# An encoder layer's second MLP product: residual filled into the accumulators by ScalarE, shared accumulators kept by copies, a last half-pass without seven-product units, and a normalisation that ends from PSUM

## The chip, the cores and the metric

The kernel runs on one core of a Trainium2 chip. The metric is the device time of one execution in microseconds (us). The kernel before took 1088.08 us, the median of three runs (1086.86 to 1090.04).

Five queues matter here, and each works strictly in the order of its own instructions: TensorE (PE, matrix products into PSUM), VectorE (DVE), ScalarE (ACT), GpSimd (POOL) and SyncE (SP, which issues the loads). [...]

## The reference, cut to what matters

One layer of a post-norm encoder on 256 tokens of width 2048, all in float32. The change is in the last third:

```python
def squared_relu_mlp(h, w_mlp_in, w_mlp_out):        # 2048 -> 8192 -> 2048
    return jnp.square(jax.nn.relu(h @ w_mlp_in)) @ w_mlp_out

x = layer_norm(ALPHA * x + xa, ln2_g[l], ln2_b[l])
ff = squared_relu_mlp(x, w_mlp_in[l], w_mlp_out[l])
x = layer_norm(ALPHA * x + ff, ln3_g[l], ln3_b[l])
```

## The kernel before, in words

**Split operands.** Every float32 operand is used as a sum of two parts, `hi` and `lo`. ACT writes `hi` (a copy rounded to the PE's format), then DVE writes `lo` (source minus `hi`). One product is then three matmuls: hi x hi, hi x lo, lo x hi (`mm3`, lines 164 to 166). A stretch of up to 1024 weight columns that is split at once is called a *part* here (`part`, `queued_split`, lines 957 and 958). `w_hi` has four buffers and `lo` four, so ACT can split a part only when PE has finished the part four before it.

**The work list.** Two kinds of items, each with one 1 MB load of weights, form one list (`items`): a *tile* ("g") makes 128 of the hidden columns, and a *unit* ("u") multiplies 256 hidden rows (a pair of tiles) into 1024 of the 2048 output columns. `step` takes the next item and `fetch` issues a load three items ahead. A tile (`hidden_tile`) is two parts, T0 and T1, and 32 matmuls. Its bank is then emptied (ACT line 876, DVE line 877). After every second tile come ReLU and square on ACT, the split of the result ("ht", lines 880 and 881), and, where the pair is needed for a seven-product unit, sums of its quarters (DVE, lines 900 to 904) and their split ("aux"). That chain is `stages`; `late_finish` and `finish` decide where it stands, and for the last pair it is put in the queues exactly where `finish` is called.

**Units.** A unit is a 2 x 2 block product. A plain unit ("P") does eight block products, 24 matmuls of 512 columns, from two parts, P0 and P1. A seven-product unit ("S") does Strassen's scheme in Winograd's form, 21 matmuls from four parts, S0 to S3; three more DVE additions (`push_sums`, tile `s_t`) make sums of weights first. A P accumulates into the banks x11, x12, x21, x22; an S into x11, x12, x21 and four more, p1, p5, p6, p7. The products shared by several results stand in those four.

**Passes.** `UNITS` names the units of eight passes. A pass goes through one quarter of the hidden rows (16 tiles, index c) and half the output columns (index q), and q runs 0, 1, 1, 0, 0, 1, 1, 0, so that two neighbouring passes share the banks. Where q changes, the banks are *closed*: ACT copies p1 to `m_t` (line 1159), and DVE adds all banks, in up to eleven operations spread over the next parts, into the residual tiles `res` (lines 1118 to 1122), the first time with the factor ALPHA. x22 is added to `res` whenever a run of P units ends. In the last pass the last four units keep their parts, so that the first row block (tokens 0 to 127) finishes before the second.

**End.** `moments` gives mean and 1/sigma of a row block; then, for five column pieces each, DVE does (x - mean) x gain (line 1266), then x 1/sigma + bias (line 1274), and SP stores the piece.

What sets the order: inside the loop nearly all PE, ACT and DVE instructions are chained in the order in which the code calls them (`queue`); `after(n, f)` calls f when n more parts have been split. What stands outside (`free_order`: emptying a tile's bank, most `stages`) is placed by the scheduler when the program is built.

Of the kernel before, what the change touches and what calls it, by code (L numbers as in the profile page):

```python
# [38 lines left out]
def encoder_kernel(ctx: ExitStack, tc: tile.TileContext, t, out):  # L39
# [54 lines left out]
    def rsqrt(src, n, scale, eps):  # L94
        v = small.tile([P, 8], F32, tag="rs_v", name="rs_v")
        nc.vector.tensor_scalar(out=v[:, :n], in0=src, scalar1=scale, scalar2=eps,
                                op0=ALU.mult, op1=ALU.add)
# [1 line left out]
        nc.gpsimd.tensor_tensor(out=r[:, :n], in0=v[:, :n], in1=mhalf[:, :n], op=ALU.pow)
# [63 lines left out]
    def mm3(ps, ah, al, bh, bl, start, stop, keep=lambda ins: ins):  # L163
        keep(nc.tensor.matmul(ps, ah, bh, start=start, stop=False))  # L164
# [1 line left out]
        keep(nc.tensor.matmul(ps, al, bh, start=False, stop=stop))  # L166
# [359 lines left out]
    def moments(st):  # L526
        mv = small.tile([P, 2], F32, tag="mv", name="mv")
        nc.vector.bn_aggr(mv, st[0][:, :st[1], :])
# [556 lines left out]
    run = {}  # L1085

    def one_pass(n):
# [8 lines left out]
        if opens:
            cols = [slice((2 * q + i) * 512, (2 * q + i + 1) * 512) for i in range(2)]
            r11, r12, r21, r22 = run["res"] = [res[b][:, cc] for b in range(NB) for cc in cols]
            whole = units if closes else units + UNITS[n + 1]
# [3 lines left out]
            run["left"][id(x22)] = 2 * (n_p - HELD) if final else 2 * (len(whole) - len(whole.lstrip("P")))
            run["total"] = dict(run["left"])
            run["fresh"] = [r11, r12, r21, r22] if c == 0 else []
            run["s"] = run["sevens"] = n_s
        r11, r12, r21, r22 = run["res"]
        left, total, fresh = run["left"], run["total"], run["fresh"]

        def mm(ps, x, hi, lo):  # L1110
            start = left[id(ps)] == total[id(ps)]
            left[id(ps)] -= 1
            mm3(ps, *x, hi, lo, start, left[id(ps)] == 0, queue)

        def merge(r, x, op=ALU.add):
            if any(r is y for y in fresh):
                fresh[:] = [y for y in fresh if y is not r]
                return nc.vector.scalar_tensor_tensor(out=r, in0=r, scalar=ALPHA, in1=x, op0=ALU.mult, op1=op)
            return nc.vector.tensor_tensor(out=r, in0=r, in1=x, op=op)

        def more(ps, op=ALU.add):
            nc.vector.tensor_tensor(out=m_t, in0=m_t, in1=ps, op=op)

        def tile_bank(it):

            i = at[0] - 1
            near = [[x for x in part_ if x[0] == "u"][:1] for part_ in (items[:i][::-1], items[i:])]
            if all(x and is_seven(x[0]) for x in near) or it[1:] == (0, LEAD):
                return x22
            behind, ahead = [sum(x[0] == "g" for x in part_[:next(  # L1130
                (j for j, x in enumerate(part_) if is_seven(x) or x[1:] == (0, LEAD)), 0)])
                for part_ in (items[:i][::-1], items[i + 1:])]
            return p7 if behind == 1 and ahead else p6 if behind and not ahead else p1

        n_unit, parts = 0, []
        while n_unit < len(units):
# [6 lines left out]
            if p in sevens:  # L1143
                if run["s"] == run["sevens"] and not final:
                    while banks:
                        banks.popleft()()
# [11 lines left out]
                if run["s"] == 0:  # L1158
                    nc.scalar.activation(m_t, p1, AF.Copy)
                    xs_done = [lambda r=r, ps=ps: merge(r, ps) for r, ps in ((r12, x12), (r11, x11), (r21, x21))]  # L1160
                    banks.extend([lambda: merge(r11, m_t), lambda: more(p6)] + xs_done * (units[-1] == "S") + [
                        lambda: merge(r22, p5), lambda: merge(r12, p5),
# [232 lines left out]
```

## Time and profile before

| | |
|---|---|
| median of three runs | 1088.08 us |
| the profiled execution, its time | 1086.87 us |
| the profiled execution, its span | 1085.1 us |
| PE busy over the span | 1069.8 us |
| DVE busy | 948.0 us |
| ACT busy | 651.3 us |
| POOL busy | 37.3 us |

The span is the time from the first to the last instruction that the profile shows, and 1.8 us of the execution lie around it. An engine is "busy" while an instruction of it runs. A share over the whole span mixes stages, so the prediction reads the second product (from 445 us on) and the end apart.

### The profile page before, as it was taken

What the parts mean: (1) busy time and instruction counts of PE and PEld (TensorE: products, weight loads), DVE (VectorE), ACT (ScalarE), POOL (GpSimd) and SP (SyncE); (2) the same over time, 40 slices, a digit from 0 to 9 for tenths busy, and PEclk for the clock granted to TensorE, in tenths of its full rate; (3) what the DMA queues carried; (4) which work ended last, traced back from release to release, by engine and by line L of the source; (5) the groups of instructions that cost most, each with busy time, mean ns of one, the idle gap of its engine ahead of it and who ended that gap; (6) DMA issues with size and microseconds to landing.
All of it is one profiled execution on the core that took longest, in us unless ns stands there. A gap on an engine that the chain in (4) does not pass through costs nothing.

```text
span 1085.1 us, 15274 instructions
## 1 busy us (share of the span) xinstructions
PE 1069.8 (99%) x5828; PEld 925.4 (85%) x5828; DVE 948.0 (87%) x1314; ACT 651.3 (60%) x949; POOL 37.3 (3%) x43
## 2 busy tenths in 40 slices
PE   9999999999999999999999999999999999999995
PEld 6988899988999878888888888888888888888885
DVE  6878677778779686889999999989999999999998
ACT  6555567546575526566756667656676656676660
POOL 2402000000000000000000000000000000000000
PEclk9999999999999999999999999999999999999998
DMA  9664454476476435765564655646555555556552
GB/s 331 232 232 136 156 192 155 156 239 222 164 248 231 179 124 187 242 224 195 193 233 156 232 195 194 223 165 231 187 203 208 188 209 211 199 192 230 193 196 78
DMA packets 37369, 215.86 MB, mean 199 GB/s; under 512 B 4272, under 2 KB 5168, under 8 KB 13616
## 3 DMA queue, kind: packets, MB, share of 16 engines
q1 hardware_dynamic: 37296, 214.89, 56.0%
q8 instruction: 45, 0.74, 0.3%
q14 instruction: 28, 0.23, 0.1%
HBM read 212.78 MB, written 2.10 MB: 198 GB/s over the span
## 4 chain that ended last, share of the span: by engine, by line
PE 93%; DVE 3%; DMA 2%; issue 1%; ACT 0%; SPq 0%; POOL 0%; DVEq 0%; ACTq 0%
PE acc L1028 15%; PE acc L165 12%; PE acc L164 12%; PE acc L166 12%; PE acc L1036 8%; PE att L164 5%; PE att L166 5%; PE att L165 5%; PE att L1028 4%; PE acc L206 2%; PE acc L204 2%; PE acc L205 2%; PE att L1036 2%; PE acc L213 1%; PE att L213 1%; DMA raw<-in_w_qa 1%
## 5 line engine op out<-in xcount | busy, mean ns | idle before, releaser
L87 ACT ACTIVATE w_hi<-raw 128x1024 fp32r<-128x1024 f32 (+2 forms) x134 | 131.5, 989 | 110.0 <-PE acc L166 74.7
L88 DVE TENSOR_TENSOR w_lo<-raw,w_hi 128x1024 fp32r<-128x1024 f32 (+2 forms) x130 | 146.0, 1132 | 53.4 <-ACT w_hi L87 52.3
L1028 PE MATMUL acc<-x2t,w_hi 128*128 128x512 f32 x688 | 178.4, 391 | 0.0
L958 DVE TENSOR_TENSOR lo<-raw,w_hi 128x1024 fp32r<-128x1024 f32 (+1 forms) x150 | 164.0, 1114 | 4.1 <-ACT w_hi L957 3.8
L957 ACT ACTIVATE w_hi<-raw 128x1024 fp32r<-128x1024 f32 (+1 forms) x150 | 142.2, 972 | 15.0 <-PE att L1028 10.0
L1028 PEld LDWEIGHTS acc<-x2t,w_hi 128*128 128x128 f32 x688 | 126.6, 189 | 22.8
L958 DVE TENSOR_TENSOR lo<-s_t,w_hi 128x1024 fp32r<-128x1024 f32 x96 | 117.1, 1220 | 15.1 <-ACT w_hi L957 14.9
L957 ACT ACTIVATE w_hi<-s_t 128x1024 fp32r<-128x1024 f32 x96 | 101.5, 1057 | 42.5 <-DVE lo L958 18.7
L1036 PEld LDWEIGHTS acc<-x2t,lo 128*128 128x128 f32 x688 | 93.9, 190 | 6.7
L1036 PE MATMUL acc<-x2t,lo 128*128 128x256 f32 x688 | 95.9, 282 | 0.0
L876 ACT ACTIVATE tmp<-acc 128x256 f32<-128x256 f32 x47 | 17.7, 385 | 117.1 <-PE acc L1028 112.7
L165 PE MATMUL acc<-w_lo,xt 128*128 128x512 f32 (+2 forms) x192 | 69.6, 364 | 0.6 <-DVE w_lo L88 0.6
L166 PE MATMUL acc<-w_hi,xt 128*128 128x512 f32 (+2 forms) x192 | 69.2, 361 | 0.0
L164 PE MATMUL acc<-w_hi,ht 128*128 128x512 f32 x174 | 67.8, 390 | 0.0
L166 PE MATMUL acc<-w_hi,ht 128*128 128x512 f32 x174 | 67.7, 389 | 0.0
L165 PE MATMUL acc<-lo,ht 128*128 128x512 f32 x174 | 67.7, 389 | 0.0
L164 PE MATMUL acc<-w_hi,xt 128*128 128x512 f32 (+2 forms) x192 | 66.0, 363 | 0.3 <-ACT w_hi L87 0.3
L165 PE MATMUL att<-lo,aux 128*128 128x512 f32 x140 | 54.5, 389 | 0.0
L166 PE MATMUL att<-w_hi,aux 128*128 128x512 f32 x140 | 54.5, 389 | 0.0
L164 PE MATMUL att<-w_hi,aux 128*128 128x512 f32 x140 | 54.5, 389 | 0.0
L1028 PE MATMUL att<-x2t,w_hi 128*128 128x512 f32 x208 | 53.9, 392 | 0.0
L165 PE MATMUL acc<-w_lo,ot 128*128 128x512 f32 (+1 forms) x136 | 51.7, 381 | 0.0
(290 smaller groups left out, 2482.3 us busy)
## 6 DMA issues: line engine op xcount, KB each, us to landing
raw<-in_w_mo SPq DMA_DIRECT2D x38, 1024.0 KB, 4.8
raw<-in_w_mc SPq DMA_DIRECT2D x35, 1024.0 KB, 4.8
raw<-in_w_out SPq DMA_DIRECT2D x16, 1024.0 KB, 4.8
row_b<-in_w_mo SPq DMA_DIRECT2D x13, 1024.0 KB, 4.9
raw_x<-in_w_mo SPq DMA_DIRECT2D x13, 1024.0 KB, 4.8
raw_x<-in_w_mc SPq DMA_DIRECT2D x12, 1024.0 KB, 4.8
row_b<-in_w_mc SPq DMA_DIRECT2D x9, 1024.0 KB, 4.8
raw<-in_w_mi SPq DMA_DIRECT2D x8, 1024.0 KB, 4.9
```

Source lines behind the costliest of these rows:

```text
L87: pin(nc.scalar.activation(hi, src, AF.Copy), pinned)
L88: return pin(nc.vector.tensor_tensor(out=lo, in0=src, in1=f(hi), op=ALU.subtract), pinned)
L164: keep(nc.tensor.matmul(ps, ah, bh, start=start, stop=False))
L165: keep(nc.tensor.matmul(ps, ah, bl, start=False, stop=False))
L166: keep(nc.tensor.matmul(ps, al, bh, start=False, stop=stop))
L204: nc.tensor.matmul(ps, hi, xt[:, k, 0:S], start=k == 0, stop=False)
L205: nc.tensor.matmul(ps, hi, xt[:, k, S:2 * S], start=False, stop=False)
L206: nc.tensor.matmul(ps, lo, xt[:, k, 0:S], start=False, stop=k == nk - 1)
L957: queue(nc.scalar.activation(hi, src, AF.Copy))
L958: queue(nc.vector.tensor_tensor(out=lo, in0=src, in1=f(hi), op=ALU.subtract))
L1028: queue(nc.tensor.matmul(ps, hi[:, k * P:(k + 1) * P], x2t[:, k0 + k, :], start=k0 + k == 0, stop=k0 + k == KT - 1))
L1036: queue(nc.tensor.matmul(ps[:, 0:S], lo[:, k * P:(k + 1) * P], x2t[:, k0 + k, 0:S], start=False, stop=False))
```

## The change

- `UNITS` goes from 48 S and 16 P to 50 S and 14 P. The last pass has eight P units and no S; every pass takes its hidden rows in plain order (`ORDERS`). In pass 6 the last tile stands before the sixth unit and not before the seventh.
- `close` replaces the additions of x11, x12 and x21 at a change of q: ACT copies the finished bank into `res` (`swap`) and fills the bank with the next residual (`seed`), so that the next matmuls add onto it. At the first change of q, DVE still adds these three banks with the factor ALPHA, and the four p banks are not added at all: ACT copies them to `row_b` and back into the banks when pass 3 opens (`kept`).
- A P unit splits both its parts first and then goes bank by bank.
- `row_b` was a fifth buffer for weight loads (`JOIN`); it no longer is.
- The end reads x11, x12, x21 and x22 in PSUM. For row block 1, the columns finished earlier are normalised on PE: gain x residual and -gain are split ahead of time, and ten matmuls with the identity and with mean x identity make (x - mean) x gain in PSUM.

```diff
-    UNITS = ["PPSSSSSS", "PPSSSSSS", "SSSSSSSP", "PSSSSSSS", "SSSSSSSP", "PSSSSSSS", "SSSSSSPP", "PSPSPPPP"]
-    TILES = ["22111111", "11111111", "11111111", "11111111", "11111111", "10111111", "11111110", "00000000"]
+    UNITS = ["PSSSSSSS", "PSSSSSSS", "SSSSSSSS", "PPSSSSSS", "SSSSSSSS", "PSSSSSSS", "SSSSSSPS", "PPPPPPPP"]
+    ORDERS = [tuple(range(CH // 2))] * len(PASSES)
+    TILES = ["22111111", "11111111", "11111111", "11111111", "11111111", "11111111", "11111100", "00000000"]
...
-            raws.append(row_b if n == JOIN else raws[n - (4 if n < JOIN else 5)])
+            raws.append(raws[n - 4])
...
+    def copy(dst, src, scale=1.0):
+        queue(nc.scalar.activation(dst, src, AF.Copy, scale=scale))
+    def seed(n, i):
+        c, q = PASSES[n]
+        copy(xs[i], quarters(q)[i], ALPHA if c == 0 else 1.0)
+    def close(n):
+        p1, p5, p6, p7 = pt
+        final = n + 1 == len(PASSES) - 1
+        rs = r11, r12, r21, r22 = quarters(PASSES[n][1])
+        def swap(i):
+            if n == 0:
+                merge(rs[i], xs[i], scale=ALPHA)
+            else:
+                copy(rs[i], xs[i])
+            seed(n + 1, i)
+        if final:
+            after(1, lambda: seed(n + 1, 3), lambda: swap(1))
+            after(2, lambda: swap(0), lambda: swap(2))
+        else:
+            after(2, lambda: swap(1), lambda: swap(0))
+            after(3, lambda: swap(2))
+        if n == 0:
+            run["p"] = kept = [row_b[:, i * 512:(i + 1) * 512] for i in range(4)]
+            copy(kept[0], p1)
+            after(4, lambda: copy(kept[1], p5), lambda: copy(kept[3], p7))
+            after(5, lambda: copy(kept[2], p6))
+            return
+        copy(m_t, p1)
+        after(2, lambda: merge(r11, m_t))
+        after(3, lambda: merge(m_t, p6), lambda: merge(r12, m_t, ALU.subtract))
+        after(4, lambda: merge(r12, p5), lambda: merge(r22, p5))
+        after(5, lambda: merge(m_t, p7, ALU.subtract))
+        after(6, lambda: merge(r22, m_t, ALU.subtract))
+        after(7, lambda: merge(r21, m_t))
...
-                for i in range(2):
-                    w = halves(part(raw[:, i * 1024:(i + 1) * 1024]))
-                    for (hi, lo), to in zip(w, ((x12, x22), (x11, x21))):
-                        for b in range(2):
-                            mm(to[b], a(c, k + i, b), hi, lo)
+                ws = [halves(part(raw[:, i * 1024:(i + 1) * 1024])) for i in range(2)]
+                for ps, b, j in ((x22, 1, 0), (x12, 0, 0), (x11, 0, 1), (x21, 1, 1)):
+                    for i in range(2):
+                        mm(ps, a(c, k + i, b), *ws[i][j])
...
-        done(0, r12, x12)
-        done(0, r11, x11)
+        copy(p1[:, 0:256], x22[:, 256:512])
+        gains()
+        for r in (x12, x11):
+            queue(stats(sts[0], r))
+        leave_first()
+        ends = ((x21, 1, 0, 512), (x22[:, 0:256], 0, 0, 256), (p1[:, 0:256], 0, 256, 256))
+        for ps, i, c0, w in ends:
+            for j, (k, hl) in enumerate(parts):
+                hi, lo = [x[:, c0:c0 + w] for x in hl[i]]
+                mm3(ps, *a(c, k, 1), hi, lo, False, j == len(parts) - 1, queue, True)
+            queue(stats(sts[1], ps))
...
+    def leave_last():
+        for hi, lo, ps in pieces:
+            for w in (hi, lo):
+                queue(nc.tensor.matmul(ps, unit, w[:, 512:1024], start=w is hi, stop=False))
+        mu, r = moments(sts[1], queue)
+        queue(nc.scalar.activation(turn_hi, ident, AF.Identity, scale=mu))
+        shift(1, mu, col(LATE), x21)
...
+        for hi, lo, ps in pieces:
+            for i, (x, w) in enumerate(((turn_hi, hi), (turn_hi, lo), (turn_lo, hi))):
+                queue(nc.tensor.matmul(ps, x, w[:, 0:512], start=False, stop=i == 2))
```

**Place 1, PE, a P unit** (the first of pass 0). `lo_4180` and `lo_4181` are the low parts of P0 and P1. In the difference, + is the change:

```order
 L164 MATMUL acc<-w_hi,ht 128x512
 L165 MATMUL acc<-lo_4180,ht 128x512
 L166 MATMUL acc<-w_hi,ht 128x512
 L164 MATMUL acc<-w_hi,ht 128x512
+L165 MATMUL acc<-lo_4181,ht 128x512
+L166 MATMUL acc<-w_hi,ht 128x512
+L164 MATMUL acc<-w_hi,ht 128x512
 L165 MATMUL acc<-lo_4180,ht 128x512
```

Before, all twelve matmuls of P0 came first; now the second block product already takes P1.

**Place 2, ACT, around the last tile of pass 6.** Before (x4 are T0 and T1 of that tile and P0 and P1 of the P unit behind it; L876 empties the tile's bank, L889 and L890 are ReLU and square, and the last row is the next P unit's two parts):

```order
L957 ACTIVATE w_hi<-raw 128x1024 x4
L876 ACTIVATE tmp<-att 128x256
L889 ACTIVATE tmp<-tmp 128x512
L890 ACTIVATE tmp<-tmp 128x512
L880 ACTIVATE ht<-tmp 128x2x256
L957 ACTIVATE w_hi<-row_b 128x1024 x2
```

In the change the unit at this place is the sixth S; the bank is emptied by L875, L888 and L889 are ReLU and square, and the last row is P0, P1 and S0 of the next two units:

```order
L875 ACTIVATE tmp<-acc 128x256
L953 ACTIVATE w_hi<-s_t 128x1024
L888 ACTIVATE tmp<-tmp 128x512
L889 ACTIVATE tmp<-tmp 128x512
L879 ACTIVATE ht<-tmp 128x2x256
L879 ACTIVATE aux<-tmp 128x512
L953 ACTIVATE w_hi<-raw 128x1024 x3
```

Before, one P unit's parts stood ahead of the chain and gave PE work while it ran. Now only the S unit's last part (`s_t`) does; P0 and P1 stand behind the chain, which has one step more, the split of the sums ("aux").

**Place 3, ACT, the first change of q** (the end of pass 0; `row_b<-att` keeps p1, `acc<-res` are seeds, `w_hi<-raw x2` are T0 and T1 of the tile, the two single `w_hi<-raw` below them P0 and P1). The change:

```order
L953 ACTIVATE w_hi<-s_t 128x1024
L1084 ACTIVATE row_b<-att 128x512
L953 ACTIVATE w_hi<-raw 128x1024 x2
L888 ACTIVATE tmp<-tmp 128x512
L889 ACTIVATE tmp<-tmp 128x512
L1084 ACTIVATE acc<-res_1484 128x512 x2
L953 ACTIVATE w_hi<-raw 128x1024
L875 ACTIVATE tmp<-att 128x256
L1084 ACTIVATE acc<-res_1485 128x512
L953 ACTIVATE w_hi<-raw 128x1024
```

Before, the same stretch (the single row ahead of L890 is P0, the pair behind it P1 and the first part of the tile after; L876 empties the first tile's bank):

```order
L1159 ACTIVATE m_t<-att 128x512
L957 ACTIVATE w_hi<-raw_x 128x1024 x2
L889 ACTIVATE tmp<-tmp 128x512
L957 ACTIVATE w_hi<-raw 128x1024
L890 ACTIVATE tmp<-tmp 128x512
L957 ACTIVATE w_hi<-raw 128x1024 x2
L876 ACTIVATE tmp<-att 128x256
```

Before, both parts of the P and one of the next tile stood ahead of the row that empties the tile's bank; now P1 stands behind that row and behind a seed.

More of the change, by code (lines that the diff above doesn't have):

```diff
@@ L1096, in one_pass @@
+        r22 = quarters(q)[3]
         if opens:
-            cols = [slice((2 * q + i) * 512, (2 * q + i + 1) * 512) for i in range(2)]
-            r11, r12, r21, r22 = run["res"] = [res[b][:, cc] for b in range(NB) for cc in cols]
-            whole = units if closes else units + UNITS[n + 1]
+            whole = units if final or closes else units + UNITS[n + 1]
             n_s, n_p = whole.count("S"), whole.count("P")
-            run["left"] = {id(ps): n_s + 2 * n_p for ps in (x11, x12, x21)}
+            run["left"] = {id(ps): n_s + 2 * n_p for ps in (x11, x12)}
+            run["left"][id(x21)] = run["left"][id(x11)]
@@ L1102, in one_pass @@
             run["left"].update({id(ps): n_s for ps in pt})
[L1103 to L1108, printed above, removed]
+            run["seeded"] = {id(ps) for ps in (x11, x12, x21)} if n else set()
@@ L1110, in mm @@
+            if final:
+                run["left"][id(x22)] = 2 * n_p
+                run["seeded"].add(id(x22))
+            run["scale"] = ALPHA if c == 0 else None
+            run["s"], run["begun"] = n_s, set()
+        left = run["left"]
+        if "kept" in run:
+            run["seeded"].update(id(ps) for ps in pt)
+            del run["kept"]
         def mm(ps, x, hi, lo):
-            start = left[id(ps)] == total[id(ps)]
+            seeded = id(ps) in run["seeded"]
+            start = not seeded and id(ps) not in run["begun"]
+            run["begun"].add(id(ps))
@@ L1112, in mm @@
             left[id(ps)] -= 1
[L1113 to L1122, printed above, removed]
@@ L1124, in tile_bank @@
-        def tile_bank(it):
[L1126 to L1133, printed above, removed]
+            mm3(ps, *x, hi, lo, start, left[id(ps)] == 0, queue, seeded)
@@ L1158, in one_pass @@
                 if run["s"] == 0:
[L1159 to L1162, printed above, removed]
[L1163 to L1164 removed]
+                    close(n)
             elif final and len(units) - n_unit < HELD:
@@ L1231, in norm_ops, with col, shift, leave @@
             for i, op in enumerate((ALU.mult, ALU.add)) for b in range(NB)]
+    g3, b3 = s_t, row_b
+    LATE, EARLY = 1024 * PASSES[-1][1], 1024 * (1 - PASSES[-1][1])
+    pieces = []
+    def col(o, w=512):
+        return slice(o, o + w)
+    def shift(b, mu, c, src=None):
+        queue(nc.vector.scalar_tensor_tensor(out=res[b][:, c], in0=res[b][:, c] if src is None else src,
+                                             scalar=mu, in1=g3[:, c], op0=ALU.subtract, op1=ALU.mult))
+    def leave(b, src, c, r):
+        queue(nc.vector.scalar_tensor_tensor(out=res[b][:, c], in0=src, scalar=r, in1=b3[:, c],
+                                             op0=ALU.mult, op1=ALU.add))
+        nc.sync.dma_start(out[b * P:(b + 1) * P, c], res[b][:, c])
@@ new lines, in gains @@
+    def gains():
+        nc.sync.dma_start(g3, t["ln3_g"].partition_broadcast(P))
+        nc.sync.dma_start(b3, t["ln3_b"].partition_broadcast(P))
+        for n in range(2):
+            o = EARLY + n * 512
+            hi, lo = wsp.tile([P, 1024], F32R, tag="w_hi", name="w_hi"), lo_tile()
+            copy(hi[:, 0:512], g3[:, col(o)], -1.0)
+            queue(nc.vector.scalar_tensor_tensor(out=lo[:, 0:512], in0=g3[:, col(o)], scalar=-1.0,
+                                                 in1=f(hi[:, 0:512]), op0=ALU.mult, op1=ALU.subtract))
+            x = res[1][:, col(o)]
+            queue(nc.vector.tensor_tensor(out=x, in0=x, in1=g3[:, col(o)], op=ALU.mult))
+            queued_split(hi[:, 512:1024], lo[:, 512:1024], x)
+            pieces.append((hi, lo, pt[1 + n]))
```

139 lines of the change are left out of this document (66 added, 73 removed).

## The prediction

> **What bounds the kernel now.** I read the page's totals first, then busy time by stretch, then what PE waited for.
>
> ```profile
> span 1085.1 us, 15274 instructions
> PE 1069.8 (99%) x5828; PEld 925.4 (85%) x5828; DVE 948.0 (87%) x1314; ACT 651.3 (60%) x949; POOL 37.3 (3%) x43
> ...
> 445.00:1046.00 601.00, 601.00 (x3063) 513.46 (x3062) 573.79 (x721) 387.93 (x504) 0.00 (x0) 1.00 0.57 203
> 1074.20:1085.10 10.90, 0.00 (x0) 0.00 (x0) 7.15 (x16) 0.00 (x0) 0.92 (x1) 0.69 0.37 138
> ...
> PE acc L213 <- ACT x2t L757: 1.6, 1, 1.6
> ...
> PE acc L164 <- ACT w_hi L87: 0.3, 1, 0.3
> ```
>
> PE is 99% busy, and through the whole second product (445 to 1046 us) it never stops; the five waits it has in the run (first and last shown) lie elsewhere. So a matmul less is time won, any new wait of PE is time lost, and behind the last matmul stands an end of 10.9 us. But DVE is busy for 573.79 of those 601.00 us: it has 4.5% to spare. What decides is how far ACT and DVE are ahead when PE wants a part. The chain of waits gives PE's beat, the timeline one S unit (the last of pass 4; a change of q follows):
>
> ```profile
> 853.69 1.81 PE acc L1028 x8
> ...
> 864.03 1.81 PE att L1028 x8
> ...
> 859.09 0.40 PE L164 MATMUL att<-w_hi,ht 128*128 128x512 f32 x1
> ...
> 859.29 0.38 ACT L876 ACTIVATE tmp<-acc 128x256 f32<-128x256 f32 x1 [2.69 <-PE acc L1028]
> 859.57 1.05 ACT L957 ACTIVATE w_hi<-s_t 128x1024 fp32r<-128x1024 f32 x1
> 860.52 0.59 ACT L1159 ACTIVATE m_t<-att 128x512 f32<-128x512 f32 x1
> 861.00 2.01 ACT L957 ACTIVATE w_hi<-raw 128x1024 fp32r<-128x1024 f32 x2
> ...
> 859.71 0.42 DVE L877 TENSOR_TENSOR tmp<-acc,tmp 128x256 f32<-128x256 f32 x1
> 860.66 1.23 DVE L958 TENSOR_TENSOR lo<-s_t,w_hi 128x1024 fp32r<-128x1024 f32 x1 [0.53 <-ACT w_hi L957]
> ...
> 862.40 1.28 DVE L1119 TENSOR_TENSOR res<-res,att 128x512 f32<-128x512 f32 x2
> 863.60 2.35 DVE L958 TENSOR_TENSOR lo<-raw,w_hi 128x1024 fp32r<-128x1024 f32 x2
> ...
> 866.47 2.35 DVE L958 TENSOR_TENSOR lo<-row_b,w_hi 128x1024 fp32r<-128x1024 f32 x2
> ```
>
> Eight matmuls in 1.81 us are 0.227 each. Tile plus S repeat every 10.34 us: S is 21 x 0.227 = 4.78, a tile the other 5.55, a P 24 x 0.227 = 5.45. I count from an S's first matmul, S+0 = 859.09. ACT empties the tile's bank from S+0.20, S3's hi follows at S+0.48, its lo is done at S+2.80. PE wants it after five block products and one matmul, 16 x 0.227 = S+3.63: **0.8 us ahead**, no more. From row to row, DVE takes 1.14 us per 1024 columns, 0.60 per 512, 0.34 per 256; ACT 0.95, 0.5 and 0.28.
>
> **The matmuls.** Two units turn from P to S: 2 x 3 matmuls x 0.227 = **-1.4 us**. DVE gains nothing by it: two S more cost it 2 x (0.60 + 1.14 split + three additions, 2.3) = 8 us, and the additions that the changes of q lose give about as much back.
>
> **P units want P1 earlier.** P1's first lo was matmul 14 of a P, and is now matmul 5: at P+0.91 and not at P+2.95. At 868.82 (the row at 866.47 ends) DVE was done with P1's lo, 3.6 us before its use; of this 2.0 go.
>
> **The changes of q.** A copy PSUM to SBUF of 512 columns is the row at 860.52, 0.48 to the next. Filling a bank (SBUF to PSUM) has no row: between this and the 0.63 of a 512-column copy in SBUF; I take 0.5, and the ends move any sum below by under 0.3. Work in order of the queues, P's first matmul at 4.78 + 5.55 = S+10.33:
>
> - *End of pass 0* (place 3): P1's split stands behind the emptying of the tile's bank, so it can't start before PE ends the tile. S+10.33 + 0.20 + 0.28 (emptying) + 0.52 (seed) + 1.05 (hi) + 1.22 (lo) = S+13.6, wanted at S+11.24: PE waits **2.4 us**.
> - *End of pass 2*: ACT does m_t (from S+1.43), T0, T1, then copy, ReLU, seed, copy, square, seed (six, 3.1 together), P0 from S+6.85 to 7.9, copy, seed, P1 to S+10.0. DVE follows: P0's lo to 9.07, m_t + p6 and r12 - m_t, the second on the first's result, to 10.4, 256 columns to 10.72, P1's lo to S+11.94, wanted at 11.24: **0.7**.
> - *End of pass 4*: the same 0.7; then only one P follows, and DVE has nine 512-column operations, three additions for the next S and four splits before that S's S1 at S+23.8, wanted at 23.65; S2 and S3 come 0.5 and 0.1 late after this: **1.5** in all. (Pass 2's end has a second P, which gives the time back.)
> - *End of pass 6*, no tile between: m_t 1.45 to 1.9, P0 to 3.0, seed, copy, seed, P1's hi to S+5.6, its lo to S+6.85. P starts at S+4.78 and wants it at 5.69: **1.2**.
>
> **The last tile** (place 2). Before, the same chain ran beside a P:
>
> ```profile
> 1020.41 0.40 PE L164 MATMUL acc<-w_hi,ht 128*128 128x512 f32 x1
> ...
> 1020.61 0.38 ACT L876 ACTIVATE tmp<-att 128x256 f32<-128x256 f32 x1 [4.50 <-PE att L1028]
> 1021.49 0.63 ACT L889 ACTIVATE tmp<-tmp 128x512 f32<-128x512 f32 x1 [0.49 <-DVE tmp L877]
> 1022.15 0.63 ACT L890 ACTIVATE tmp<-tmp 128x512 f32<-128x512 f32 x1
> 1022.82 0.63 ACT L880 ACTIVATE ht<-tmp 128x512 fp32r<-128x512 f32 x1
> 1023.36 2.00 ACT L957 ACTIVATE w_hi<-row_b 128x1024 fp32r<-128x1024 f32 x2
> ...
> 1024.43 2.36 DVE L958 TENSOR_TENSOR lo<-row_b,w_hi 128x1024 fp32r<-128x1024 f32 x2 [0.26 <-ACT w_hi L957]
> ```
>
> There the next part's split began 2.95 us after PE's last matmul of the tile had made way, its lo ended at 1025.6, and PE took it at 1026.1: 0.5 us to spare, with 5.45 us of P to cover it. Now the cover is an S of 4.78 us whose own last part (0.95) goes first, and the sums come in between, as these rows show elsewhere (DVE's steps wait for each other, and ACT's "aux" for the last):
>
> ```profile
> 461.46 0.42 DVE L900 TENSOR_TENSOR tmp<-tmp 128x256 f32<-128x256 f32 x1
> 461.91 0.29 DVE L903 TENSOR_TENSOR tmp<-tmp 128x128 f32<-128x128 f32 x1
> 462.24 0.29 DVE L904 TENSOR_TENSOR tmp<-tmp 128x128 f32<-128x128 f32 x1
> ...
> 454.37 0.63 ACT L880 ACTIVATE aux<-tmp 128x512 fp32r<-128x512 f32 x1 [0.72 <-DVE tmp L904]
> ```
>
> ACT: ReLU from S+1.43, square 2.09, ht 2.76 to 3.39. DVE: ht's lo 3.42 to 4.03, the three sums to 5.10. ACT: aux 5.13 to 5.65, P0's hi to 6.7; DVE P0's lo to S+7.95. PE wanted it at 4.78 + 0.23 = 5.01: 2.95 late. Then `s_t`'s first addition (1.14) stands ahead of P1's lo, which ends at 10.23 and is wanted 0.68 after P0's: 1.6 more. Together **4.6 us**, the largest term.
>
> **Smaller waits.** Pass 0 has its first S one unit earlier, while DVE still does the ln2 rows and two pairs' chains; by the order of its queue and the times per row above, S2's lo comes some 0.4 late, an estimate. With 0.1 at a P elsewhere: **0.5**.
>
> **The end.**
>
> ```profile
> 1073.88 0.28 PE L166 MATMUL acc<-wide,ht 128*128 128x256 f32 x1
> ...
> 1074.20 0.42 DVE L1205 TENSOR_TENSOR res<-res,acc 128x256 f32<-128x256 f32 x1
> ...
> 1074.93 0.42 DVE L524 BATCH_NORM_STATS2 bn<-res 128x6 f32<-128x256 f32 x1
> 1075.39 0.29 DVE L528 BATCH_NORM_AGGREGATE mv<-bn 128x2 f32<-128x30 f32 x1
> ...
> 1077.11 0.74 DVE L1274 SCALAR_TENSOR_TENSOR res<-res,rs_r,raw 128x512 f32<-128x512 f32 x1
> 1077.77 0.74 DVE L1266 SCALAR_TENSOR_TENSOR res<-res,mv,s_t 128x512 f32<-128x512 f32 x1
> ...
> 1080.55 0.87 DVE L1274 SCALAR_TENSOR_TENSOR res<-res,rs_r,raw 128x256 f32<-128x256 f32 x2
> ...
> 1076.01 0.92 POOL L99 TENSOR_TENSOR rs_r<-rs_v,mhalf 128x1 f32<-128x1 f32 x1 [7.76 <-DVE rs_v L96]
> ```
>
> PE's last matmul ends at 1074.16 = E. Before: addition, a leftover piece of block 0, statistics, the aggregate at E+1.23, the first use of 1/sigma at E+2.95, the last piece at E+7.26, and 3.7 us of store. Now no addition; block 0 is done before E; the aggregate at E+0.45, so 1/sigma at E+2.2; meanwhile one shift of 512 and two of 256 with a small one, to E+2.7; then three pieces of 512 (0.67) and two of 256 (0.40) to E+5.5. Of the ten matmuls four fit in the first 0.9 us, six follow the mean and end near E+3, a piece or two before DVE reads them. **-1.8 us**; if PE's six came late, nothing would be won: 0.
>
> **Sum.** -1.4 - 1.8 + 2.4 + 0.7 + 1.5 + 1.2 + 4.6 + 0.5 = +7.7. On the profiled execution's own time, 1086.87, that is 1094.6; the median of the runs is 1.2 higher, so 1095.8 there. I say **1095**.
>
> **Rivals.**
>
> 1. *No wait is new; the kernel is faster.* Then only -3.2 is left: 1084.9, or 1083.7 from the profiled time. It decides at the last tile: P0's lo must be there by S+5.0, so ACT would have to split P0 by S+3.8 and not 6.7, and the order of its queue forbids it. 0.06.
> 2. *Only the last tile and the last change of q cost*, since the three waits at the other changes lie within 0.7 to 2.4 us and each needs ten to twenty rows to add up rightly: -3.2 + 4.6 + 1.2 = +2.6, 1090. For it: PE had no wait at any change before. Against: P1 is wanted 2 us earlier at each. 0.17.
> 3. *The waits let PE's clock drop.* The windows of the end:
>
> ```profile
> 1077.00:1081.00 4.00, 0.00 (x0) 0.00 (x0) 4.00 (x9) 0.00 (x0) 0.00 (x0) 0.66 0.35 133
> 1081.00:1085.10 4.10, 0.00 (x0) 0.00 (x0) 0.42 (x2) 0.00 (x0) 0.00 (x0) 0.50 0.35 128
> ```
>
>    Half clock is the floor, and 0.66 over 4 us puts the drop 1.3 us after 1077.0, so 4.1 us after PE's last matmul. My longest wait is 3 us, so no drop; were there one, matmuls take twice 0.227 until it ends: some 4 us of that, by the time it took to fall, would cost 2, and twice 4: 1099. 0.09. [...]
> 4. *Loads come late*, since four buffers are left of five.
>
> ```profile
> raw<-in_w_mo SPq DMA_DIRECT2D x38, 1024.0 KB, 4.8
> ```
>
>    A load lands in 4.8 us, and a buffer comes round every four items, some 20 us, so none should be late. If some were, the time would lie above 1099. 0.04.
>
> **How the numbers follow.** My forecast, with each wait off by up to a third (1091.5 to 1099), gets 0.64; the rivals 0.06, 0.17, 0.09, 0.04. The range 1089.5 to 1099 leaves out the first, the fourth and part of the second and third. 0.3% (3.3 us) is about what a measurement of this kernel can tell: faster means below 1084.8, slower above 1091.3. Rival 1 gives faster 0.05 and same 0.01; rival 2 same 0.14 and slower 0.03; the rest is slower but for 0.02.
>
> **What would show it.** PE waits for `lo` (L165's successor) or `w_hi` in the second product, five places, the longest at the first P behind the last tile; PE's last 256-column matmul some 9.5 us later; from there to the end of the span 9.1 us and not 10.9. If PE shows no wait there, I am wrong about the queues; if waits are short but the time is long, about the clock.

## The result, and the profile after

| | before | after |
|---|---|---|
| median, runs taken side by side (five each) | 1087.38 us (1086.75 to 1090.04) | 1104.63 us (1102.88 to 1105.48) |
| ratio, 95% interval | | 1.0153 (1.0137 to 1.0169) |
| span of the profiled execution | 1085.1 us | 1103.1 us |

The kernel is 17 us slower, where 8 were forecast. The page's totals:

```profile
span 1103.1 us, 15327 instructions
PE 1079.9 (98%) x5832; PEld 928.1 (84%) x5832; DVE 946.9 (86%) x1310; ACT 672.2 (61%) x992; POOL 36.6 (3%) x43
```

DVE has as much to do as before (948.0 us), ACT 21 us more; neither is full over the span. What PE waited for (in total, how often, the longest; `acc` and `att` are the kernel's PSUM tiles of 128x512 float32, four buffers of each, its banks):

```profile
PE acc L165 <- DVE lo L954: 5.8, 7, 1.3
PE acc L164 <- ACT w_hi L953: 3.0, 2, 1.8
PE att L165 <- DVE lo L954: 2.7, 3, 1.7
PE acc L213 <- ACT x2t L757: 1.6, 1, 1.6
```

The last line stood there before; the first three are new, and all three are splits that come late in the second product. Windows of the same trace (the columns are busy time of PE, PEld, DVE, ACT, POOL, then the granted clock, DMA share, GB/s):

```profile
445.00:1046.00 601.00, 590.26 (x2992) 501.10 (x2991) 564.69 (x709) 396.04 (x528) 0.00 (x0) 0.99 0.57 201
...
396.50:402.00 5.50, 3.93 (x14) 3.16 (x13) 4.24 (x9) 2.15 (x4) 0.00 (x0) 0.69 0.00 0
476.00:492.00 16.00, 12.44 (x60) 9.65 (x59) 14.81 (x21) 10.36 (x15) 0.00 (x0) 1.00 0.43 144
551.00:559.00 8.00, 6.00 (x21) 4.37 (x20) 6.16 (x10) 5.71 (x9) 0.00 (x0) 0.79 0.38 126
1031.00:1040.00 9.00, 5.14 (x15) 3.29 (x14) 7.95 (x12) 3.99 (x5) 0.00 (x0) 0.82 0.23 67
```

Two things stand in these windows. In pass 0 (476 to 492) PE is idle for 3.6 of 16 us. And in three windows the granted clock is below 1 (0.69, 0.79 and 0.82), so that the matmuls are slow as well as late.

The difference of the spans, 18.0 us, can be laid out place by place: each gap between the starts of neighbouring matmuls beyond the usual 0.227 us, added up. (The rounded places add up to 18.1.)

| place | forecast | measured |
|---|---|---|
| matmuls saved | -1.4 | -1.4 |
| end | -1.8 | -1.3 |
| pass 0's first two S units | +0.4 | **+4.4** |
| end of pass 0 | +2.4 | +2.55 |
| end of pass 2 | +0.7 | +0.86 |
| end of pass 4 | +1.5 | +1.6 |
| last tile | +4.6 | +4.7 |
| end of pass 6 | +1.2 | +1.6 |
| half clock, three places (1.6 at 398 us, 1.6 at the end of pass 0, 1.4 at the last tile) | 0 | **+4.6** |
| start of the kernel, and waits elsewhere | +0.1 | +0.5 |
| sum | +7.7 | +18.1 |

**Pass 0.** ACT's timeline, then DVE's, then PE's at the first two S units:

```profile
474.56 0.63 ACT L879 ACTIVATE aux<-tmp 128x512 fp32r<-128x512 f32 x1 [4.52 <-DVE tmp L903]
475.36 2.00 ACT L953 ACTIVATE w_hi<-s_t 128x1024 fp32r<-128x1024 f32 x2
...
475.65 1.22 DVE L1255 TENSOR_TENSOR res<-res,row_b 128x1024 f32<-128x1024 f32 x1
477.72 2.35 DVE L954 TENSOR_TENSOR lo<-s_t,w_hi 128x1024 fp32r<-128x1024 f32 x2
...
487.81 0.42 DVE L876 TENSOR_TENSOR tmp<-acc,tmp 128x256 f32<-128x256 f32 x1 [1.07 <-ACT tmp L875]
489.28 0.68 DVE L954 TENSOR_TENSOR lo<-raw,w_hi 128x512 fp32r<-128x512 f32 x1
490.49 2.35 DVE L954 TENSOR_TENSOR lo<-s_t,w_hi 128x1024 fp32r<-128x1024 f32 x2
...
478.99 0.50 PE L165 MATMUL att<-lo,aux 128*128 128x512 f32 x1 [1.74 <-DVE lo L954]
490.02 0.50 PE L165 MATMUL acc<-lo,ht 128*128 128x512 f32 x1 [1.05 <-DVE lo L954]
491.76 0.50 PE L165 MATMUL att<-lo,aux 128*128 128x512 f32 x1 [0.76 <-DVE lo L954]
```

At the first S, PE waits for the `lo` of S2 (the row at 477.72). ACT's side of it, S2 and S3 (`w_hi<-s_t`), stands behind "aux", which waits 4.52 us for DVE's quarter sums (L903), but it is done at 477.36 all the same. DVE shows no wait from 464.26 to 486.70 (22.19 of 22.44 us busy) and comes to that row straight from the rows ahead of it, an ln2 row (L1255) among them. So DVE's backlog alone sets this wait.

At the second S, DVE has caught up. It waits 1.07 us for the emptying of the tile's bank (487.81), which can't start before PE has ended the tile at 487.36. The rest of the pair's chain and then S1's `lo` (489.28) stand behind that row, and S2's (490.49) behind these: PE waits twice.

**Last tile.** PE's timeline:

```profile
1031.30 0.39 PE L166 MATMUL acc<-w_hi,ht 128*128 128x512 f32 x1
1033.50 0.50 PE L164 MATMUL acc<-w_hi,ht 128*128 128x512 f32 x1 [1.81 <-ACT w_hi L953]
1034.76 0.51 PE L165 MATMUL acc<-lo,ht 128*128 128x512 f32 x1 [0.76 <-DVE lo L954]
1035.10 0.40 PE L166 MATMUL acc<-w_hi,ht 128*128 128x512 f32 x1
1035.34 0.40 PE L164 MATMUL acc<-w_hi,ht 128*128 128x512 f32 x1
1037.03 0.79 PE L165 MATMUL acc<-lo,ht 128*128 128x512 f32 x1 [1.29 <-DVE lo L954]
1037.62 0.63 PE L166 MATMUL acc<-w_hi,ht 128*128 128x512 f32 x1
1038.05 0.63 PE L164 MATMUL acc<-w_hi,ht 128*128 128x512 f32 x1
```

The waits are for hi of P0, lo of P0 and lo of P1: the three waits of the forecast, at the forecast place, 4.7 us together. Behind them matmuls start 0.43 us apart and not 0.227.

**The end.** DVE's aggregate and its last step behind PE's last 256-column matmul, which starts at 1093.27 (its end, E, is 1093.55):

```profile
1094.06 0.29 DVE L528 BATCH_NORM_AGGREGATE mv<-bn 128x2 f32<-128x30 f32 x1
...
1097.48 1.53 DVE L1271 SCALAR_TENSOR_TENSOR res<-att,rs_r,row_b 128x512 f32<-128x512 f32 x3
```

DVE is done at E+5.46 (forecast E+5.5). The stores took 4.1 us from there and not 3.7, so 1.3 is left of the 1.8.

### The profile page after: what moved, and what is told of

Same layout as the page of the kernel before. It is cut to its first block, busy times and chain, and to the rows that moved or that the text cites. A ratio compares the mean times of both kernels' runs of the same rounds, so it can differ in the third digit from the quotient of the medians.

```text
span 1103.1 us, 15327 instructions
## 1 busy us (share of the span) xinstructions
PE 1079.9 (98%) x5832; PEld 928.1 (84%) x5832; DVE 946.9 (86%) x1310; ACT 672.2 (61%) x992; POOL 36.6 (3%) x43
## 4 chain that ended last, share of the span: by engine, by line
PE 89%; DVE 5%; ACT 2%; DMA 2%; issue 1%; SPq 0%; DVEq 0%; POOL 0%; ACTq 0%
PE acc L1024 16%; PE acc L165 12%; PE acc L166 11%; PE acc L164 11%; PE acc L1032 8%; PE att L165 4%; PE att L166 4%; PE att L164 4%; PE acc L206 2%; PE acc L204 2%; PE acc L205 2%; DVE lo L954 2%; PE acc L213 1%; PE att L213 1%; ACT w_hi L953 1%
## 5 line engine op out<-in xcount | busy, mean ns | idle before, releaser
L1024 PE MATMUL acc<-x2t,w_hi 128*128 128x512 f32 x800 | 207.4, 391 | 0.0
L954 DVE TENSOR_TENSOR lo<-raw,w_hi 128x1024 fp32r<-128x1024 f32 (+1 forms) x182 | 190.8, 1071 | 13.9 <-ACT w_hi L953 13.9
L953 ACT ACTIVATE w_hi<-raw 128x1024 fp32r<-128x1024 f32 (+1 forms) x182 | 165.0, 935 | 18.7 <-PE acc L166 12.0
L1024 PEld LDWEIGHTS acc<-x2t,w_hi 128*128 128x128 f32 x800 | 147.2, 189 | 26.5
L1032 PEld LDWEIGHTS acc<-x2t,lo 128*128 128x128 f32 x800 | 109.1, 190 | 7.8
L1032 PE MATMUL acc<-x2t,lo 128*128 128x256 f32 x800 | 111.6, 282 | 0.0
L875 ACT ACTIVATE tmp<-acc 128x256 f32<-128x256 f32 x54 | 20.4, 384 | 132.5 <-PE acc L1024 128.2
L954 DVE TENSOR_TENSOR lo<-raw_x,w_hi 128x1024 fp32r<-128x1024 f32 x58 | 70.5, 1218 | 3.3 <-ACT w_hi L953 3.3
L946 DVE TENSOR_TENSOR s_t<-s_t,raw 128x512 f32<-128x512 f32 x100 | 68.5, 685 | 0.9
L953 ACT ACTIVATE w_hi<-raw_x 128x1024 fp32r<-128x1024 f32 x58 | 60.6, 1053 | 4.0 <-PE acc L166 2.3
L946 DVE TENSOR_TENSOR s_t<-raw 128x1024 f32<-128x1024 f32 x50 | 60.9, 1217 | 0.0
```

What stands on the lines that cost most here:

```text
L946: sums.append(lambda: queue(nc.vector.tensor_tensor(out=out, in0=a, in1=b, op=ALU.add)))
L953: queue(nc.scalar.activation(hi, src, AF.Copy))
L954: queue(nc.vector.tensor_tensor(out=lo, in0=src, in1=f(hi), op=ALU.subtract))
L1024: queue(nc.tensor.matmul(ps, hi[:, k * P:(k + 1) * P], x2t[:, k0 + k, :], start=k0 + k == 0, stop=k0 + k == KT - 1))
L1032: queue(nc.tensor.matmul(ps[:, 0:S], lo[:, k * P:(k + 1) * P], x2t[:, k0 + k, 0:S], start=False, stop=False))
```

## The experiments

All are built from the changed kernel; each median is compared with its 1104.63, and each ratio with the 1.0153 above. Kernels of one group ran beside the kernel before on one chip, which took 1087.7, 1087.16 and 1087.15 us there. Gaps between matmuls are added up as in the table above.

### Four single edits

**The last pair's chain behind the P of pass 6.**

```diff
     def finish():
+        if late_finish and late_finish[0][1:] == (NCH - 1, CH // 2 - 1) and at[0] < items.index(("u", NCH - 1, 1, 7)):
+            return
```

> One edit: the last tile's chain (ReLU, square, splits, sums) is put behind the P unit that follows the sixth S of pass 6, not ahead of its splits. In the changed kernel PE lost 6.3 us there (waits of 2.0, 1.0, 1.8 and half clock). Theory A (the order of ACT's queue makes this wait): P0 and P1 are split in time, some 0.2 us of waiting is left at the P, and up to 1.5 us moves to the S behind it, whose sums come later: 4 to 6 us faster than the changed kernel, 1099 to 1101 us. Rival B (DVE is simply full, a wait taken away here comes back within the next units): within 2 us of the changed kernel's 1104.6.

Measured 1097.92 (1097.51 to 1101.63), ratio 1.0100 (1.0082 to 1.0119), 6.7 us less, rather more than theory A's 4 to 6, and against rival B. At the last tile the gaps fall from 4.7 to 1.5 us and the clock stays full (outside the gaps the matmuls start 0.23 us apart); the half clock at 398 us is absent too (a granted clock of 1.00 from 396.5 to 402 us), which is not the edit's doing (last section). The place of the chain in the queues is the cause of the largest term.

**A P unit in the order of its parts**, all of P0's products and then P1's, as before the change.

```diff
-                for ps, b, j in ((x22, 1, 0), (x12, 0, 0), (x11, 0, 1), (x21, 1, 1)):
-                    for i in range(2):
+                for i in range(2):
+                    for ps, b, j in ((x22, 1, 0), (x12, 0, 0), (x11, 0, 1), (x21, 1, 1)):
                         mm(ps, a(c, k + i, b), *ws[i][j])
```

> One edit: in a P unit PE takes all block products of P0 first, then those of P1, bank order kept. Theory A (P1 is wanted 2 us too early): the waits at the first P after a change of q go where slack follows: end of pass 0 4.2 to 0.4 us with no half clock, end of pass 2 0.9 to 0; end of pass 4 keeps its sum of 1.6 (DVE's backlog reaches the S behind); behind the last tile only the 3.0 for P0 is left of 6.3; the last change of q keeps about 0.9 for banks not filled yet. Some 8 us faster than the changed kernel, 1096 to 1097. Rival C (ACT's bank fills and copies are what PE waits for, in whatever order it takes the parts): under 2 us faster.

Measured 1099.52 (1097.19 to 1102.83), ratio 1.0118 (1.0097 to 1.0138), 5.1 less, between the two theories' numbers. The gaps at the end of pass 0 fall from 2.55 us, and 1.6 of half clock, to 0.6, with a granted clock of 1.00 from 551 to 559 us; at the end of pass 2 from 0.86 to none; at the last tile P1's wait of 1.5 is gone and P0's two stay. Of the 6.6 us of gaps at the four changes of q, 3.1 stay. So asking for P1 two microseconds sooner accounts for about half of them, and for the half clock behind the first. In pass 0 the gaps grew by 0.7.

**Passes 0 and 1 start with two P units**, as before.

```diff
-    UNITS = ["PSSSSSSS", "PSSSSSSS", "SSSSSSSS", ...
+    UNITS = ["PPSSSSSS", "PPSSSSSS", "SSSSSSSS", ...
```

With it (not shown) go the quarter sums of the second pair of tiles and their split, which no S needs then.

> One edit: passes 0 and 1 begin with two P units, as before, so two units turn from S to P (6 matmuls, 1.4 us more) and the second pair of tiles needs no sums. Theory A (the first S comes while DVE and ACT still work off the start): the waits of 4.3 us in pass 0 go: 2.9 us faster than the changed kernel, 1101.7. Rival B: the waits move to the first S behind, and the kernel is 1 to 2 us slower. If the half clock seen at 398 us, ahead of any changed instruction, hangs on this edit, another 1.4 us goes.

Measured 1102.37 (1099.62 to 1103.04), ratio 1.0129 (1.0113 to 1.0145). In the trace pass 0's 4.4 us are gone to the last tenth; 1.4 of matmuls come back, and the half clock at the last tile, which came again, lasted longer and cost 2.9 us and not 1.4 (the mean granted clock of this profile is 0.992, of the changed kernel's 0.995). The 4.4 us of pass 0, theory A's place for them, went; 2.9 of them were given back, half by the matmuls and half by the clock.

**No filling of the banks.**

```diff
     def seed(n, i):
         c, q = PASSES[n]
-        copy(xs[i], quarters(q)[i], ALPHA if c == 0 else 1.0)
+        return
```

The output lacks the residual then, so this is a probe and no cure.

> One edit: the copies that fill banks with the residual are left out, so that a bank goes on from what it held and the output lacks the residual. The copies out stay. Theory A (order of queues): where a fill stands ahead of P1's split it goes 0.5 us earlier per fill: end of pass 2 0.9 to 0, end of pass 0 half a us of 2.5 and perhaps its 1.6 of half clock, last change of q 1.0 of 1.6, last tile nothing, pass 0 nothing: 2.5 to 4.5 us faster than the changed kernel, 1100 to 1102. Rival C (the fills are the cause): all waits at the changes of q go, 8 us, 1096.5.

Measured 1096.69 (1095.57 to 1097.20), ratio 1.0080 (1.0065 to 1.0095), 7.9 less: rival C's number, and more than theory A allowed. The gaps at the changes of q went, all but 0.2 us. ACT's timeline at the end of pass 0, of the changed kernel and then of this one, shows how fills of 0.6 us can cost that:

```profile
548.47 1.04 ACT L953 ACTIVATE w_hi<-raw 128x1024 fp32r<-128x1024 f32 x1
551.89 0.38 ACT L875 ACTIVATE tmp<-att 128x256 f32<-128x256 f32 x1 [2.37 <-PE att L1024]
552.17 0.60 ACT L1084 ACTIVATE acc<-res 128x512 f32<-128x512 f32 x1
552.69 1.04 ACT L953 ACTIVATE w_hi<-raw 128x1024 fp32r<-128x1024 f32 x1
```

```profile
546.09 1.05 ACT L953 ACTIVATE w_hi<-raw 128x1024 fp32r<-128x1024 f32 x1
...
550.85 0.38 ACT L875 ACTIVATE tmp<-att 128x256 f32<-128x256 f32 x1 [1.29 <-PE att L1024]
```

With fills, P1 (552.69) stands behind the row that empties the tile's bank, and this one waits 2.37 us for PE to end the tile. Without them P1 (546.09) stands ahead of it. A fill costs little by itself; the place that it takes in the queue puts P1 on the wrong side of a wait.

### The edits together, and a look at pass 0

**The first two together.**

> Both single cures together (the last chain behind P0 of pass 6, and a P unit in the order of its parts); pass 0 stays as in the changed kernel. Theory A (PE waits at six separate places, each set by what stands ahead in ACT's and DVE's queues, and the clock halves behind the longest of them): the two cures act on different waits, so they add. What is left is pass 0's first two S units, 4.3 us, and about 1.5 us of small waits: 1087.7 - 1.4 (matmuls) - 1.4 (end) + 4.3 + 1.5 = 1090.7, range 1089.5 to 1092.5, and full clock from 545 to 1046 us. Rival D (DVE is 95% busy, so a wait cured at one place comes back at the next): no more than 2 us below the better of the two alone, 1096 to 1098.

Measured 1096.56 (1095.74 to 1098.78), ratio 1.0088 (1.0073 to 1.0103). Theory A's sum is missed by 5.9 us, and D's number came out, though not for D's reason: at the changes of q and the last tile the cures hold side by side. I had put the small waits left over at 1.5 us; they are 0.6 (end of pass 0), 1.5 (pass 4), 1.5 (last tile) and 0.5 (pass 6). Pass 0 has 5.2 us of gaps and not 4.4, and there, this time, the clock halved, for 1.6 (granted: 0.59 from 478 to 482 us).

**All three together.**

> As the kernel with both cures, and passes 0 and 1 start with two P again, as before the change (two more matmul triples, +1.4 us, and one stage less for pair 1's chain at the start). Theory A: pass 0's 4.3 us go too; 1087.7 - 1.4 (end) + 1.5 (small waits) = 1087.8, range 1086.5 to 1089. Rival D (waits come back elsewhere): 1093 or more.

Measured 1090.17 (1089.29 to 1091.65), ratio 1.0028 (1.0016 to 1.0039), 1.2 above theory A's range and well below D's: 14.5 of the 17 us are undone. Pass 0 has no gap left. The medians leave 3.0 us above the kernel before, the profiled spans 4.5 (1089.6 against 1085.1): the small waits just named, 4.1, and half clock, 1.5 (the mean granted clock of the profile is 0.997), less the end's 1.3, make 4.3 of it.

**The second half of the ln2 rows later**, with the first two edits.

```diff
     for i, x in enumerate(norm_ops(1)):
-        after(2 * i + 6, x)
+        after(2 * i + 24, x)
```

> As the kernel with both cures, and the four multiplications and additions of the second half of the ln2 rows (1.14 us each on DVE) come 18 parts later, behind the first S units of pass 0. Theory A (DVE's sums come late because of its backlog, ACT's splits of S2 and S3 stand behind a split that waits for these sums): DVE is up to 4.6 us further at 477 us, the first S's wait of 1.9 goes, of the second S's 2.1 some stays: 1087 to 1089, 2 to 4 us below the kernel with both cures. Rival E (the order of ACT's queue alone sets it, with the emptying of the tile's bank in it, not DVE's backlog): within 1 us of the kernel with both cures.

Measured 1096.31 (1095.02 to 1097.63), ratio 1.0083 (1.0068 to 1.0097): nothing won, which is rival E's number. The trace shows that its reason is another. The first S unit's gaps, 2.8 us in the kernel with the two edits, are gone, as theory A has it. But the four rows now stand between 495.56 and 512.93, beside the third and the fourth S, and at the fourth a gap of 2.6 us has opened, with half clock behind it (matmuls 0.43 us apart from 512.55). DVE's timeline and PE's (PE waits for the first `lo` of the row at 509.78):

```profile
505.12 1.22 DVE L1257 TENSOR_TENSOR res<-res,row_b 128x1024 f32<-128x1024 f32 x1
...
509.78 1.82 DVE L954 TENSOR_TENSOR lo<-raw,w_hi 128x1024 fp32r<-128x1024 f32 x2
511.71 1.22 DVE L1257 TENSOR_TENSOR res<-res,row_b 128x1024 f32<-128x1024 f32 x1
...
511.05 0.50 PE L165 MATMUL att<-lo,ht 128*128 128x512 f32 x1 [2.43 <-DVE lo L954]
```

So DVE's backlog did set the first S unit's wait, against rival E; but DVE had no room for the rows at the later place either, and moving them moved the wait.

**The first two pairs' sums split two parts later**, beside that.

```diff
-            after(n + 3, halve_sums)
+            after(n + 5, halve_sums)
```

> As the kernel before it in this call, and the splits of the sums of the first two pairs come two parts later in the queues, behind the S unit's own splits. Theory A: the second S's waits (1.2 and 0.9) shrink as well: 0.5 to 2 us below that kernel, 1085.5 to 1088, the first version at or below the kernel before. Rival E' (the S unit's splits stand behind the emptying of the tile's bank, which PE ends only as the S begins): within 0.5 us of it.

Measured 1095.26 (1094.43 to 1096.09), ratio 1.0074 (1.0061 to 1.0088), 1.05 us less, which these medians can't tell from nothing, and far from theory A's 1085.5 to 1088. At the second S one of its two gaps shrank from 0.95 to 0.34 us. The other, 1.2 us, stayed: there rival E' is right, since S1's `lo` still stands behind the emptying of the tile's bank in DVE's queue.

### The clock, and the tile's place

**Eight matmuls whose result is not used**, in the first wait behind the last tile.

```diff
+                if n == len(PASSES) - 2:
+                    for i in range(8):
+                        queue(nc.tensor.matmul(x22, x2t[:, i, 0:P], x2t[:, i, :], start=i == 0, stop=i == 7))
                 for ps, b, j in ((x22, 1, 0), (x12, 0, 0), (x11, 0, 1), (x21, 1, 1)):
```

> The changed kernel with eight matmuls of 512 columns more, ahead of the one P of pass 6 behind the last tile, into the bank of x22, which the P begins anew: their result is not used, and their operands have long been there. Theory W (the clock halves when PE stood idle for most of some 3 us): eight times 0.227 = 1.8 us of work fill the first of the three waits there (1.97 us) and leave the second and third (1.0, 1.4 us) as they are; P's own matmuls start no earlier and no later, and run 0.227 apart instead of 0.427 for the first 2.7 us: 1.2 us less at this place, and no granted clock below 1.0 between 1030 and 1042 us. Rival R (the clock falls by chance, or by what the splits do, and not by PE's idle time): matmuls 0.427 apart behind the waits as before, time unchanged; the eight matmuls then run into the P, and nothing is gained.

PE's timeline there (L1222 is the added line):

```profile
1028.76 1.98 PE L1222 MATMUL acc<-x2t 128*128 128x512 f32 x8
1030.73 0.50 PE L164 MATMUL acc<-w_hi,ht 128*128 128x512 f32 x1
1031.99 0.50 PE L165 MATMUL acc<-lo,ht 128*128 128x512 f32 x1 [0.76 <-DVE lo L954]
...
1034.26 0.50 PE L165 MATMUL acc<-lo,ht 128*128 128x512 f32 x1 [1.29 <-DVE lo L954]
1034.60 0.40 PE L166 MATMUL acc<-w_hi,ht 128*128 128x512 f32 x1
1034.84 0.39 PE L164 MATMUL acc<-w_hi,ht 128*128 128x512 f32 x1
...
1028.00:1040.00 12.00, 9.95 (x42) 7.37 (x41) 9.23 (x14) 5.50 (x7) 0.00 (x0) 1.00 0.34 109
```

The idle times of 0.76 and 1.29 us are those of the changed kernel to the hundredth, and the last matmuls stand 0.24 apart where they were 0.43; the granted clock is 1.00. That is as theory W has it, 1.4 us less at this place, though in one profile (the last section has more). The median, 1104.07 (1100.81 to 1105.41), ratio 1.0149 (1.0129 to 1.0169), can't tell so little from nothing.

**The last tile one unit earlier**, with the second and third edit.

```diff
-    TILES = [..., "11111100", "00000000"]
+    TILES = [..., "11112000", "00000000"]
...
-            return x22 if is_seven(items[at[0]]) or it[1:] == (0, LEAD) else p1
+            return x22 if is_seven(next(x for x in items[at[0]:] if x[0] == "u")) or it[1:] == (0, LEAD) else p1
```

> As the kernel with all three cures, but the last pair's chain is not held back; instead the last tile comes one unit earlier (two tiles ahead of unit 4 of pass 6, both into the bank of x22), so that an S lies between the tile and the two units that need the chain. Theory A (the last tile's wait is the distance between the tile and the first unit whose splits stand behind the chain): the 2.07 us of PE's waits between 1029 and 1038 us shrink to under 1, with 0.5 new at the second tile, which waits for its bank: 1088.5 to 1089.5 (1090.2 with all three cures). Rival D (DVE is full there: three S and a P without a tile to cover them give the wait back at the last S): 1090 or more, with waits for lo of 1 to 3 us at unit 5 or 7.

Measured 1098.09 (1097.64 to 1099.26), ratio 1.0097 (1.0080 to 1.0114), 8 us above the kernel with all three cures, so theory A fell; D's wait came (3.0 us), with more beside it. The second and third edit alone were not run. PE's timeline at the unit behind the first S:

```profile
1022.35 0.49 PE L164 MATMUL att<-w_hi,ht 128*128 128x512 f32 x1 [1.81 <-ACT w_hi L953]
1025.86 0.79 PE L165 MATMUL att<-lo,ht 128*128 128x512 f32 x1 [3.01 <-DVE lo L954]
```

Two S units now follow each other with the chain between them, and no tile gives DVE time. The second tile also waited 1.5 us for its bank, where I had said 0.5.

**The same with two P units at the start of pass 0 only.**

> As that kernel, but only pass 0 starts with two P; pass 1 starts with one (three matmuls fewer, 0.7 us, and one more stage of pair 1's chain at the start). Theory A (pass 0's waits come from the first S standing one unit too early; pass 1 has no such need): 0.7 us below that kernel. Rival D (DVE's load of 4 us more for one more S comes out as a wait in pass 0 or 1): 1 us or more above it.

Measured 1098.13 (1096.74 to 1098.40), ratio 1.0096 (1.0081 to 1.0111): no difference from the one before. Its pass 1 shows no new wait, so D is out; the 0.7 us of theory A is less than these medians can tell.

No version beat the kernel before; the one with all three cures came closest.

## Why the prediction was wrong

The direction was right, the time lay 5.6 us above the range. By the prediction's steps:

- **Matmuls** and **the end**: -1.4 and -1.3, as forecast but for 0.5 us, most of it the store.
- **The changes of q**: 5.8 forecast, 6.6 measured. The working by queue order held to 0.4 us at each. The experiments confirm both parts of it: P1 is asked for too soon (the order of parts takes 3.5 us of the 6.6 away), and fills stand in its way (all but 0.2 go without them). That P1 stands behind the emptying of the bank because of the fills was read from the rows at the end of pass 0.
- **The last tile**: 4.6 forecast, 4.7 measured, and 3.2 of it gone when the chain is moved.
- **Smaller waits** is the first step that failed: "S2's lo comes some 0.4 late" was 2.0 us at the first S, and the second S, put at nothing, cost 2.4 more. At the first the cause was the one named, DVE's backlog, and its size was wrong; the prediction doesn't give the rows that it counted, so what it missed there stays open. At the second it is the order of DVE's queue behind the emptying of the tile's bank. With two P at the start of pass 0 this cost is 0, in all four kernels that have them; one of these (two P in pass 0 only) keeps the sums of the second pair, so it is the place of the first S that counts.
- **Rival 3, the clock**, is the second: it failed in its condition, was counted at 0.09, and stood in the sum at nothing. I read from the end of the kernel that the clock falls 4.1 us after PE's last matmul, and said that no wait of 3 us could do it. It fell behind waits of 1.4 and 1.0 us with one matmul between. It cost 4.6 us in the profiled execution, at three places. One of them, 1.6 us at 398 us, lies ahead of any changed instruction and is luck: of the profiles of eight kernels, two have it (a granted clock of 0.69 from 396.5 to 402 us) and six do not (1.00). In the profile of the changed kernel half clock followed where PE was idle for 1.93 to 2.27 us of a window of 3.41 us (last section). The 4.1 us are the rest of one such window, 0.74 us, and one that was wholly idle; they don't say how long a wait must be.

The sum missed by 18.0 - 7.7 = 10.3 us: 4.6 are the clock, 4.0 pass 0, and 1.7 all other terms together. Had either of the two come as forecast, the profile's own time (1086.87 + 18.0, less the one) would still be 1100.3 or 1100.9, a little above the range; only without both it would lie inside, at 1096.3.

- **Rivals 1, 2 and 4**: all places forecast to wait did wait, so 1 and 2 are out; PE waited for no load in the second product, so 4 is out.

What stays open: what opens the small waits at the end of pass 4 (1.5 us in every version but the one without fills) was read from rows and not tried by itself. The same holds for the order that sets the second S unit's waits in pass 0.

## What to carry to other kernels

Where two engines feed a third in fixed order, follow the instruction that is needed through both queues, and ask of each row ahead of it what that row waits for. Carry a backlog past the first unit that feels it: here the second unit lost as much as the first. An edit that seems to cost its own duration (a fill of 0.6 us) can cost several times that if it shifts a needed split behind a row that waits. And count a new PE wait with what the clock may add: short waits close together brought 1.4 to 1.6 us of half clock with them here, and in one profile, with matmuls of no use in the first of three waits, it stayed full (1.00).
